# Further semaphore waits on three engines of a ReLU row-sum kernel

## The chip, the cores and the metric

The kernel runs on one core of a Trainium2 chip. The metric is the device time of one execution in microseconds (us). A core has five engines that run their own instruction streams: TensorE (PE), VectorE (DVE), ScalarE (ACT), GpSimd (POOL) and SyncE (SP). They are ordered by semaphores only: an instruction or a transfer raises a semaphore when it is done, and another engine's instruction waits until the semaphore has reached a value. Data comes from device memory (HBM) to the on-chip memory (SBUF, 128 partitions) by 16 DMA engines.

## The reference

```python
def setup_inputs():
    batch, seq, dim = 32, 512, 1024
    return {"x": np.random.randn(batch, seq, dim).astype(np.float32)}

def reference(x):
    relu_x = np.maximum(x, 0)
    return np.sum(relu_x, axis=-1).astype(np.float32)
```

The input is 16,384 rows of 1,024 float32 values (67.1 MB), the output one float32 for each row: negative values count as zero, and the row is summed.

## The kernel before

The 16,384 rows are laid out as 128 partitions with 128 rows each. Rows come in as seven chunks of 16 rows for each partition (8 MiB a chunk; the first chunk in two transfers), then a tail of 8, 4 and 2 rows, and the last two rows in four pieces (three into `buf`, one into `seam`). `buf` has three chunk buffers (`NB = 3`).

SyncE issues every transfer, from one queue. Chunks 0 to 2 are issued at once (L91), those of chunk 0 being moved ahead of the program's opening barrier (L96). For chunk c from 3 on, SyncE first waits for `s_dve` to reach `done[c - 3]` (L87), that is until VectorE's reductions of the chunk that used this buffer are done; `done` is 3, 6, 9, 12, 15, 18. The wait ahead of the tail's transfers (c = 7 in the loop) is of the same kind. A transfer raises its own semaphore `s_in[c]` by 16 when it has landed; there are 13 of these: seven chunks, three pieces of the tail, three of the last rows. Then SyncE issues the tail (L101), the last rows (L112, L115), and the three stores of results (L117, L123, L207), each behind the waits that it needs. The last line of the program, L209, waits for the stores to land.

For chunks 0 to 5, ScalarE takes most rows through a ReLU in place (L145), raising `s_act`, and VectorE sums them by a reduction over each row (L160), 18 reductions in all, each raising `s_dve` by one. Some rows of a chunk are done by one engine alone, ReLU and sum in one instruction (L127 on ScalarE, L130 on VectorE). From chunk 6 on both engines take rows in turn in this second way. A row whose values come in different pieces at the very end is put together in `seam`.

TensorE has no instruction of the kernel itself but the opening barrier's; GpSimd writes four constants and takes part in that barrier. Both are then at the end of their streams. The barrier, and what else the launch code puts in, stands under L223.

Of the kernel before, what the change touches and what calls it, by code (L numbers as in the profile page):

```python
# [6 lines left out]
NB = 3  # L7
REGIONS = [1, 111, 16]
CHUNKS = [[(0, 0, 1), (1, 0, 15)]] + [[(1, 16 * c + 15, 16)] for c in range(6)]
# [2 lines left out]
TAIL = [8, 4, 2]  # L12
CUT = 912
HEAD = 256


def bass_relu_sum_kernel(
# [19 lines left out]
    B, S, _ = x.shape  # L37
    J = B * S // P
    NBIG = len(CHUNKS)
# [12 lines left out]
    w = D - CUT  # L52
    seam = nc.alloc_sbuf_tensor("seam", [P, 2 + w + HEAD + 2], fp32)
    res = nc.alloc_sbuf_tensor("res", [P, J], fp32)
# [3 lines left out]
    s_in = [nc.alloc_semaphore(f"s_in{i}") for i in range(n_in)]  # L58
    s_act = nc.alloc_semaphore("s_act")
    s_dve = nc.alloc_semaphore("s_dve")  # L60
# [7 lines left out]
    s_out = nc.alloc_semaphore("s_out")  # L68

    sp, act, dve = nc.sync, nc.scalar, nc.vector  # L70

    NTWO = len(ACT_STEPS)
    done = [sum(map(len, DVE_STEPS[: c + 1])) for c in range(NTWO)]
# [8 lines left out]
        for i, ins in enumerate(code)  # L82
        if ins.engine == mybir.EngineType.SP and type(ins).__name__ == "InstDrain"
    )
    for c in range(NBIG + 1):
        if c >= NB:
            sp.wait_ge(s_dve, done[c - NB])  # L87
        if c < NBIG:
            i = 0
            for g, j, n in CHUNKS[c]:  # L90
                sp.dma_start(  # L91
                    out=buf[:, c % NB, i : i + n, :], in_=xv[g][:, j : j + n, :]
                ).then_inc(s_in[c], 16)
                i += n
                if c == 0:
                    code.insert(arrival, code.pop())  # L96
                    arrival += 1
    r = 0
    tail = []
    for i, n in enumerate(TAIL):  # L100
# [8 lines left out]
    flat = buf[:, tb, r : r + 2, :].rearrange("p j d -> p (j d)")  # L109
    first, second, third = [(0, CUT), (D + D // 2, 2 * D), (D + HEAD, D + D // 2)]  # L110
    for k, (lo, hi) in enumerate((first, second, third)):
        sp.dma_start(out=flat[:, lo:hi], in_=rows[:, lo:hi]).then_inc(  # L112
            s_in[NBIG + len(TAIL) + k], 16
        )
    sp.dma_start(out=seam[:, 2 : 2 + w + HEAD], in_=rows[:, CUT : D + HEAD]).then_inc(s_seam, 16)  # L115
    sp.wait_ge(s_turn, 1)
# [9 lines left out]
    def on_act(t, acc):  # L126
        return act.activation(t, t, AF.Relu, accum_out=acc)  # L127

    def on_dve(t, acc):
        return dve.tensor_scalar(  # L130
            out=t, in0=t, scalar1=0.0, scalar2=None, op0=ALU.max, op1=ALU.add, accum_out=acc
        )
# [4 lines left out]
    k = 0  # L137
# [54 lines left out]
    k = 2 + w  # L192
    lo, hi = second
    act.wait_ge(s_in[-2], 16)
    on_act(flat[:, lo:hi], seam[:, k + HEAD : k + HEAD + 1]).then_inc(s_seam, 1)
    lo, hi = third
    dve.wait_ge(s_in[-1], 16)
    on_dve(flat[:, lo:hi], seam[:, k + HEAD + 1 : k + HEAD + 2]).then_inc(s_seam, 1)
    act.wait_ge(s_seam, 16 + 2)
    act.wait_ge(s_half, 2)  # L200
    on_act(seam[:, 0:k], res[:, J - 2 : J - 1]).then_inc(s_last, 1)
    dve.wait_ge(s_seam, 16 + 2)
    on_dve(seam[:, k : k + HEAD + 2], res[:, J - 1 : J]).then_inc(s_last, 1)


    sp.wait_ge(s_last, 2)
    sp.dma_start(out=ov[-1][:, :], in_=res[:, start[-1] : J]).then_inc(s_out, 16)  # L207
# [30 lines left out]
```

## Time and profile before

| what | value |
|---|---|
| time, median of 3 runs | 160.86 us (160.74 to 161.05) |
| span of the profiled execution (first to last instruction of the program) | 159.4 us |
| instructions in the span | 150 |
| bytes read from HBM | 67.11 MB |
| ScalarE waiting for transfers at L145 | 46.1 us, 6 times |
| SyncE waiting for VectorE's reductions at L91 | 101.6 us, 4 times |
| SyncE waiting for a transfer at L122 | 31.0 us |

The span counts from the program's first instruction to its last; the time of a run is a little longer, as it holds what the launch puts around the program. An engine's busy time leaves out instructions that only wait or issue transfers, so SyncE shows no busy time at all. In the lines of the profile "q1" and "q14" are DMA queues, with packets, megabytes and the share of sixteen DMA engines' time; a name such as `SPq` or `PEldq` means an engine's sequencer, that is an instruction that waits, branches or issues. `buf<-in_x_dram` is a transfer from the input into `buf`. Lines of a timeline give the start and the length in us, the engine, the line of the kernel, the operation, what it writes and reads, and in brackets how long the engine had been idle and what ended that.

### The profile page before, as it was taken

The page shows a single profiled execution, that of the slowest core. Times are in us where ns is not written, and L with a number is a line of the kernel's source. Part 1 is how long each engine was busy: PE and PEld are TensorE (multiplying, and loading weights), DVE is VectorE, ACT ScalarE, POOL GpSimd, SP SyncE. Part 2 cuts the span into 40 slices and gives each one's busy share as a digit, 9 for nine tenths or more (in the row PEclk, how much of TensorE's full clock was granted, in tenths as well). Part 3 has the DMA queues.
Part 4 walks back from the last instruction along what each step waited for, and adds up shares of the span by engine and source line. Part 5 has one row for each costly group of instructions (what it writes and reads, how often), then busy time and mean ns, then how long its engine had stood idle before and what let it go on. Part 6 is the DMA issues. An engine that isn't in the chain of part 4 may idle for free.

```text
span 159.4 us, 150 instructions
## 1 busy us (share of the span) xinstructions
DVE 120.6 (76%) x59; ACT 101.5 (64%) x54; POOL 0.2 (0%) x4
## 2 busy tenths in 40 slices
DVE  0000000009999999999999999999999999898995
ACT  3000059980799708996099941999329980496975
POOL 0000000000000000000000000000000000000000
DMA  9997996996996997989979969969969979798994
GB/s 378 493 401 339 493 526 263 526 526 263 526 493 296 526 444 345 526 378 411 526 312 477 526 263 526 526 263 526 526 263 526 444 345 526 321 469 374 417 400 142
DMA packets 2457, 67.18 MB, mean 421 GB/s; under 512 B 536, under 2 KB 792, under 8 KB 1176
## 3 DMA queue, kind: packets, MB, share of 16 engines
q1 hardware_dynamic: 2456, 67.18, 98.1%
q14 instruction: 1, 0.01, 0.0%
HBM read 67.11 MB, written 0.07 MB: 421 GB/s over the span
## 4 chain that ended last, share of the span: by engine, by line
DVE 55%; DMA 34%; ACT 9%; SPq 2%; issue 0%
DVE res L160 54%; DMA buf<-in_x_dram 34%; ACT buf L145 9%; SPq L101 1%; SPq L112 1%; DVE buf L130 0%; DVE seam L130 0%; SPq L91 0%; DVE turned L169 0%
## 5 line engine op out<-in xcount | busy, mean ns | idle before, releaser
L160 DVE TENSOR_REDUCE res<-buf 128x4 f32<-128x4096 f32 (+3 forms) x18 | 99.4, 5596 | 35.5 <-ACT buf L145 35.5
L145 ACT ACTIVATE buf<-buf 128x7168 f32<-128x7168 f32 (+5 forms) x13 | 80.4, 6233 | 46.1 <-DMA buf<-in_x_dram 46.1
L127 ACT ACTIVATE buf<-buf 128x1024 f32<-128x1024 f32 (+2 forms) x19 | 19.0, 999 | 8.9 <-DMA buf<-in_x_dram 8.9
L130 DVE TENSOR_SCALAR_CACHE_REDUCE buf<-buf 128x1024 f32<-128x1024 f32 (+2 forms) x19 | 20.7, 1143 | 1.7 <-DMA buf<-in_x_dram 1.6
L127 ACT ACTIVATION_READ_ACCUMULATOR buf<-buf 128x1 f32 x19 | 3.6, 188 | 0.0
L145 ACT ACT_TABLE_LOAD x1 | 1.3, 1283 | 1.3 <-PEq L223 1.3
L130 DVE DVE_READ_ACCUMULATOR buf<-buf 128x1 f32 x19 | 1.6, 84 | 0.0
L130 DVE TENSOR_SCALAR_CACHE_REDUCE seam<-seam 128x258 f32<-128x258 f32 x1 | 0.4, 421 | 0.0
L127 ACT ACTIVATE seam<-seam 128x114 f32<-128x114 f32 x1 | 0.3, 300 | 0.1
L169 DVE STREAM_TRANSPOSE turned<-res 128x32 f32<-128x32 f32 x1 | 0.2, 211 | 0.0
L127 ACT ACTIVATION_READ_ACCUMULATOR seam<-seam 128x1 f32 x1 | 0.2, 186 | 0.0
L223 POOL MEMSET const-bfloat16-1.0<- 128x1 bf16 x1 | 0.1, 101 | 0.0
L223 POOL MEMSET const-uint8-127<- 128x1 uint8 x1 | 0.1, 101 | 0.0
L223 POOL MEMSET const-float32-0.0<- 128x1 f32 x1 | 0.1, 98 | 0.2 <-issue 0.2
L223 POOL MEMSET const-float32-1.0<- 128x1 f32 x1 | 0.1, 98 | 0.0
L130 DVE DVE_READ_ACCUMULATOR seam<-seam 128x1 f32 x1 | 0.1, 82 | 0.0
## 6 DMA issues: line engine op xcount, KB each, us to landing
buf<-in_x_dram SPq DMA_DIRECT2D x1, 7680.0 KB, 21.1
buf<-in_x_dram SPq DMA_DIRECT2D x1, 4096.0 KB, 25.3
buf<-in_x_dram SPq DMA_DIRECT2D x1, 2048.0 KB, 29.9
buf<-in_x_dram SPq DMA_DIRECT2D x1, 1024.0 KB, 31.9
buf<-in_x_dram SPq DMA_DIRECT2D x1, 512.0 KB, 3.3
buf<-in_x_dram SPq DMA_DIRECT2D x1, 456.0 KB, 32.5
buf<-in_x_dram SPq DMA_DIRECT2D x1, 256.0 KB, 32.7
seam<-in_x_dram SPq DMA_DIRECT2D x1, 184.0 KB, 32.6
```

What stands on the lines that cost most here:

```text
L101: sp.dma_start(out=buf[:, tb, r : r + n, :], in_=xv[-1][:, r : r + n, :]).then_inc(s_in[NBIG + i], 16)
L112: sp.dma_start(out=flat[:, lo:hi], in_=rows[:, lo:hi]).then_inc(s_in[NBIG + len(TAIL) + k], 16)
L127: return act.activation(t, t, AF.Relu, accum_out=acc)
L130: return dve.tensor_scalar(out=t, in0=t, scalar1=0.0, scalar2=None, op0=ALU.max, op1=ALU.add, accum_out=acc)
L145: act.activation(t, t, AF.Relu).then_inc(s_act, 1)
L160: dve.tensor_reduce(out=res[:, c * BIG + r : c * BIG + r + n], in_=buf[:, c % NB, r : r + n, :], axis=X, op=ALU.add,).then_inc(s_dve, 1)
L169: dve.transpose(out=turned[:, :], in_=res[:, 0:32]).then_inc(s_turn, 1)
L223: nc = _bacc.Bacc("TRN2", target_bir_lowering=False, num_devices=1)
```

## The change

A helper adds `n` waits for one semaphore and value to an engine's stream. SyncE gets 28 such calls behind the issue of each of chunks 3, 4, 5 and 6, for the value of `s_dve` that the same turn of the loop has just waited for. TensorE gets 12 for each of the 13 `s_in`, in their order, for the value that says that the piece has landed. GpSimd gets 8 for each of the 18 values of `s_dve`, in order. The compiled program has 56 to 78 further wait instructions on each of the three engines. No other instruction is added, removed or moved.

```diff
+FILL_SP = 28
+FILL_PE = 12
+FILL_POOL = 8
...
     sp, act, dve = nc.sync, nc.scalar, nc.vector
+    pe, pool = nc.tensor, nc.gpsimd
...
+    def fill(engine, n, s, v):
+        for _ in range(n):
+            engine.wait_ge(s, v)
+
     for c in range(NBIG + 1):
         if c >= NB:
             sp.wait_ge(s_dve, done[c - NB])
...
                 if c == 0:
                     code.insert(arrival, code.pop())
                     arrival += 1
+        if NB <= c < NBIG:
+            fill(sp, FILL_SP, s_dve, done[c - NB] if c >= NB else 0)
     r = 0
     tail = []
...
+    for c, s in enumerate(s_in):
+        fill(pe, FILL_PE, s, 16 * len(CHUNKS[c]) if c < NBIG else 16)
+    for k in range(done[-1]):
+        fill(pool, FILL_POOL, s_dve, k + 1)
```

## The prediction

> **What bounds the kernel now.** I began with the page's lines on DMA and the chain of work in order of time, because a kernel that reads 67 MB and writes almost nothing may simply be limited by its transfers.
>
> ```profile
> DVE 120.6 (76%) x59; ACT 101.5 (64%) x54; POOL 0.2 (0%) x4
> q1 hardware_dynamic: 2456, 67.18, 98.1%
> q14 instruction: 1, 0.01, 0.0%
> ```
>
> The reader is to see that no engine is busy for the whole span, that the data queue fills 98.1% of sixteen DMA engines' time, and that one more transfer, of instructions, lies inside the span. TensorE has no line, and GpSimd has four MEMSETs. The page's chain runs mostly over VectorE (54%), which looks as if VectorE were the limit. The timeline of ScalarE says otherwise:
>
> ```profile
> 40.97 13.95 ACT L145 ACTIVATE buf<-buf 128x7168 f32<-128x7168 f32 x2 [5.50 <-DMA buf<-in_x_dram]
> 60.31 13.95 ACT L145 ACTIVATE buf<-buf 128x7168 f32<-128x7168 f32 x2 [5.39 <-DMA buf<-in_x_dram]
> 79.67 13.95 ACT L145 ACTIVATE buf<-buf 128x7168 f32<-128x7168 f32 x2 [5.41 <-DMA buf<-in_x_dram]
> 99.02 14.04 ACT L145 ACTIVATE buf<-buf 128x4096 f32<-128x4096 f32 x3 [5.40 <-DMA buf<-in_x_dram]
> ```
>
> Every chunk of 8 MiB arrives 19.34 to 19.36 us after the one before, and ScalarE waits some 5.4 us for each: 8.389 MB / 19.35 us = 434 GB/s, or 27.1 GB/s for each of sixteen DMA engines, from about 1 us to 157 us without a hole. The end of the chain is a transfer too:
>
> ```profile
> 124.39 32.60 DMA buf<-in_x_dram
> 156.99 0.02 issue
> 157.01 0.44 DVE buf L130 x2
> 157.45 0.02 issue
> 157.47 0.43 DVE seam L130 x2
> ```
>
> So what counts is (1) anything that takes bandwidth from the stream, (2) anything that lets the stream run dry, which only SyncE can do, as it issues all transfers, and (3) what follows the last landing. Beyond the span of 159.4 us the time has 160.86 - 159.4 = 1.46 us. The records of semaphore updates in the same trace, which no view prints, show what this is: a hand-over from engine to engine at 159.51 to 159.67, resets of the semaphores by all five engines until 160.23, and a second hand-over that ends at 160.85. The last such update ahead of the program stands at -0.01, and 160.85 + 0.01 is the median, 160.86; so I take this execution's own time as 160.86, and count the hand-overs and resets.
>
> **The change, part by part.** Nothing is removed or moved. Three engines get instructions.
>
> *Number.* SyncE: 28 calls x 4 chunks = 112; TensorE: 12 x 13 semaphores = 156; GpSimd: 8 x 18 values = 144. Half of these is 56, 78 and 72, the numbers announced, so two waits share an instruction, as they do at L122 and L209. Each is worth one EVENT_SEMAPHORE:
>
> ```profile
> L223 POOLq EVENT_SEMAPHORE  x2: 17/17/17, 1.1 to 1.1; - x2
> L223 SPq EVENT_SEMAPHORE  x1: 17/17/17, 1.2 to 1.2; - x1
> L223 PEldq EVENT_SEMAPHORE  x1: 51/51/51, 1.2 to 1.2; - x1
> ```
>
> Two in a row on GpSimd start 0.08 us apart in the trace's records (1.07 and 1.15), so I take 0.08 us for SyncE and GpSimd, and 0.11 us for TensorE (its 51 ns instead of 17).
>
> *SyncE.* 14 instructions stand behind each of the issues at 52.86, 70.11, 87.58 and 104.82: 14 x 0.08 = 1.1 us. They wait for the value that the chunk's own issue has just waited for, so they only pass. Queued behind them is the wait for the next buffer, which ends 16.9 to 17.5 us after each issue. Without this cover there would still be the queue: chunk 4 is issued at 70.11 and its turn comes at 79.67, 9.6 us of slack, and more later. Cost 0.
>
> *TensorE.* It has no work; behind its waits stands only the closing hand-over. Its last six instructions wait for the last piece of buf at 156.99 and are through at 156.99 + 6 x 0.11 = 157.65. The hand-over can't be finished before SyncE has seen the last store land (the span's end, 159.4): 1.7 us of cover. Cost 0.
>
> *GpSimd.* Its last four wait for the eighteenth reduction (137.3): through by 137.6. Behind them is the hand-over again, 21 us of cover. Cost 0. No engine that computes gets an instruction, and a wait changes no semaphore, so VectorE and ScalarE have nothing more to wait for.
>
> *What is left: the code itself.* 206 instructions must be brought to the sequencers. Windows on the DMA view show how that looks. From 0 to 159 us there is q1 alone; ahead of the span there are 13 instruction packets; and the one inside lies at its very end, in a window of 20 ns (159.20 to 159.22):
>
> ```profile
> q14 instruction: 13, 0.05, 1.5%
> ...
> q14 instruction: 1, 0.01, 154.1%
> ```
>
> 154.1% of 16 x 0.02 us is 0.49 us for one packet of 8 KB (16384 GB/s in a fortieth of that window, 0.5 ns). VectorE (61 records of ours), ScalarE (57) or SyncE (22) reached that point; TensorE (2) and GpSimd (8) had not asked for any in all the 158 us that they stood. After the change they have 80 and 80, and SyncE 78: more than any engine had. If about 60 instructions made one engine fetch, all three will fetch, and in the midst of the stream: SyncE near its last fill (105 us), GpSimd near its fourteenth value of s_dve (some 110 us), TensorE near its tenth semaphore (155 us).
>
> The trace of before shows no fetch beside the stream, so its price is bounded. At the least nothing: the landings of the last piece of seam are spread over 156.98 to 157.45 by DMA engine, and a fetch on an early one disappears. One fetch that takes only its share of bandwidth on the latest engine costs 8192 B / 27.1 GB/s = 0.30 us; with the packet's own time it costs 0.49. Three on one DMA engine cost 3 x 0.49 = 1.48. A gain below nothing has no place here, since the stream has no hole to lose. The nearest rows are the single packet's two, 0.30 and 0.49, and I take the middle, 0.40 us, since three fetches on separate DMA engines delay the last landing by the latest alone.
>
> [...]
>
> *Sum.* 159.4 + 0.40 + 1.46 = 161.26 us, or 161.25.
>
> **The rivals.**
> *No change that can be measured* (within 0.2%, 0.32 us, which is about what a measurement of this kernel can tell from none). The fetches miss the stream, or land on DMA engines that finish early: 0 to 0.3 us, time 160.9 to 161.15. For it: sixteen landings spread over 0.47 us, of which only the late ones have less than 0.30 to give. Against it: three fetches, not one. I put 160.95.
>
> *Faster.* The mechanism is the fetch at the end. It runs from 159.21 to 159.70, 0.3 us past the span's end, in the midst of the hand-over. If it is SyncE's, or if an engine's closing code is late because it was not yet there, 56 to 78 more instructions have it brought during the run. The price: the 1.46 us outside the span shrink by at least 0.30 (what stands out of the span), at most by the 0.8 us between TensorE's release at 159.67 and its start of the second hand-over at 160.50. Less 0.2 for fetches in the stream, that gives 160.2 to 160.75; I put 160.35. It decides once 0.5 us are saved behind the span. For it: TensorE is, by the order of updates, the engine that opens each hand-over and the last to reset. Against it: the engines go from release to first reset in 0.11 to 0.18 us, which leaves little room for a wait for code.
>
> *Slower by a stall.* SyncE's own last instructions (the store at 157.93, the wait at L209) fall on a point where code must come, and nothing covers them: one packet, 0.49, and the some 0.9 us from SyncE's last issue (158.27) to a packet (159.21) as a delay of such a request: +1.4, 162.3. For it: SyncE would have 78 instructions, close to TensorE's 80. Against it: before, no engine shows such a stop.
>
> *The change does less than it says*: waits that are dropped as doubled. The numbers announced are exactly half of the calls, so no more than pairing was done; this goes with no change.
>
> **How the numbers follow.** Forecast (fetches cost the stream 0.3 to 0.9 us): 0.38; stall: 0.05; no change: 0.30; faster: 0.27. So slower by over 0.2% has 0.43, within 0.2% 0.30, faster 0.27. The predicted time is the forecast's 161.25. Its own range is 161.15 to 161.8. Below, the range must take in all of no change and half of faster, down to 160.2; above, it ends at 161.8, since three fetches on one engine and the stall together have less than 0.1.
>
> **What would show it.** Right: instruction packets of q14 inside the stream; chunks still 19.35 us apart but one or two of them late by 0.3 or more; the last landing near 157.8; the part outside the span still 1.46. Wrong: q14 still with one packet in the span (no change); a span of 159.4 with less than 1.2 us outside of it (faster); a gap on SyncE behind 157.4 (stall). If SyncE's issues at 70.11 to 122.07 move by more than the reductions that release them, my zero for its fills falls. If TensorE's or GpSimd's waits were found still running at 159.4, so would theirs.

## The result, and the profile after

The changed kernel takes 162.36 us (162.33 to 162.46, 5 runs) against 160.93 for the kernel before (5 runs): ratio 1.0093, 95% interval 1.0081 to 1.0105, or 1.43 us slower. The forecast was slower, 161.25 us; the measured time lies above its range.

The page of the changed kernel, in the lines that answer to those shown of before:

```profile
span 160.5 us, 356 instructions
...
DVE 120.6 (75%) x59; ACT 101.5 (63%) x54; POOL 0.2 (0%) x4
...
q1 hardware_dynamic: 2456, 67.18, 97.5%
q14 instruction: 1, 0.01, 0.0%
```

There are 206 instructions more, no engine computes longer, and there is again one instruction packet (not at the end, as before, but in the stream, as shown below). But the span is 1.1 us longer. Its end is no longer SyncE's wait for the last store: it now ends with TensorE's added waits. In the groups by source line (durations in ns, then first and last start in us), the last line of the kernel before, the same line in the changed kernel, and the added waits are these:

```profile
L209 SPq EVENT_SEMAPHORE  x1: 28/28/28, 159.4 to 159.4; - x1
```

```profile
L225 SPq EVENT_SEMAPHORE  x1: 28/28/28, 159.8 to 159.8; - x1
```

```profile
L92 PEldq EVENT_SEMAPHORE  x78: 51/51/51, 138.4 to 160.4; - x78
L92 POOLq EVENT_SEMAPHORE  x72: 42/43/43, 95.2 to 138.0; - x72
L92 SPq EVENT_SEMAPHORE  x52: 28/28/28, 53.3 to 106.0; - x52
```

L225 is the old end of the program (L209 in the kernel before). (Of SyncE's 56 further instructions four stand under L96, the line of its own wait for the next buffer.) TensorE, which computes nothing, starts its last wait at 160.4, 0.6 us after it. The same view holds the reason: TensorE's first wait is passed only at 138.4 us and GpSimd's first at 95.2, although the source gives TensorE waits from the first chunk on. TensorE's 156 waits, which nothing stands between, are 78 instructions of two, and its records show how they were paired here: the first call with the last, the second with the last but one, and so on, the innermost pair coming first. TensorE's instructions wait for semaphores (6, 6), (7, 5), (8, 4), ... (12, 0), and so 12 instructions, not 6, stand at each of the last six semaphores and none at the first six. The group narrowed to the time from 155.3 us on, when the last tail piece had landed, counts what was left:

```profile
L92 PEldq EVENT_SEMAPHORE  x48: 51/51/51, 155.3 to 160.4; - x48
```

48 in 5.1 us, 0.107 us each: from there on TensorE never waits for data, it works off a queue.

The stream is late too. ScalarE's timeline (start, length, and in brackets how long it was idle), first of the kernel before:

```profile
118.36 10.63 ACT L145 ACTIVATE buf<-buf 128x3072 f32<-128x3072 f32 x3 [5.31 <-DMA buf<-in_x_dram]
...
137.72 1.06 ACT L127 ACTIVATE buf<-buf 128x1024 f32<-128x1024 f32 x1 [6.65 <-DMA buf<-in_x_dram]
```

Then of the changed kernel:

```profile
99.18 14.04 ACT L156 ACTIVATE buf<-buf 128x4096 f32<-128x4096 f32 x3 [5.36 <-DMA buf<-in_x_dram]
118.53 10.63 ACT L156 ACTIVATE buf<-buf 128x3072 f32<-128x3072 f32 x3 [5.31 <-DMA buf<-in_x_dram]
...
138.42 1.06 ACT L138 ACTIVATE buf<-buf 128x1024 f32<-128x1024 f32 x1 [7.18 <-DMA buf<-in_x_dram]
```

Chunk 5 came 19.35 us after chunk 4, but chunk 6 took 19.89, where it had taken 19.36 before. In between lies the instruction packet, which a window of 0.1 us (137.2 to 137.3) on the DMA view finds:

```profile
q14 instruction: 1, 0.01, 19.3%
```

19.3% of 16 x 0.1 us is 0.31 us of one DMA engine. The chain ends 0.47 us later (before: 157.45 and 157.47 in the last two lines):

```profile
157.45 0.02 issue
157.47 0.45 DVE buf L141 x2
157.92 0.02 issue
157.94 0.43 DVE seam L141 x2
```

What follows the span is read from the records of semaphore updates, which no view prints. The table has us from the span's start. As these records show it, a hand-over runs from TensorE over the other engines to SyncE and back, one semaphore step each. The engines are named by the order of the steps, which is an inference; it fits that TensorE's step follows 0.19 us on its last wait in every run with waits on TensorE.

| run | last landing | SyncE's last instruction ends | TensorE opens the hand-over | SyncE's step | VectorE's step back | second hand-over ends |
|---|---|---|---|---|---|---|
| before | 157.44 | 159.39 | 1.48 | 159.51 | 159.55 | 160.85 |
| changed | 157.92 | 159.87 | 160.65 | 160.79 | 161.30 | 162.56 |
| TensorE alone | 157.50 | 159.44 | 160.22 | 160.36 | 160.87 | 162.13 |
| the same, VectorE 4 more | 157.71 | 159.68 | 160.27 | 160.41 | 160.50 | 161.77 |
| SyncE alone | 157.52 | 159.48 | 1.48 | 160.00 | 160.04 | 161.35 |
| GpSimd alone | 157.82 | 159.76 | 1.49 | 159.88 | 159.92 | 161.22 |
| fewer, TensorE in order | 157.49 | 159.44 | 158.12 | 159.55 | 159.60 | 160.86 |

Most profiled runs' own times end 0.10 to 0.12 us ahead of the last column (162.46 for the changed kernel). Three things are new in the second row: TensorE opens late, VectorE takes 0.51 us from SyncE's step to its own step back, where in the second hand-over it takes 0.10, and the last landing is late. The row with four waits more on VectorE also shows that the last landing can be some 0.25 us late without a packet in the stream, so one run's landing says little alone. The experiments take the three things apart.

### The profile page after: what moved, and what is told of

Same layout as the page of the kernel before. It is cut to its first block, busy times and chain, and to the rows that moved or that the text cites. A ratio compares the mean times of both kernels' runs of the same rounds, so it can differ in the third digit from the quotient of the medians.

```text
span 160.5 us, 356 instructions
## 1 busy us (share of the span) xinstructions
DVE 120.6 (75%) x59; ACT 101.5 (63%) x54; POOL 0.2 (0%) x4
## 4 chain that ended last, share of the span: by engine, by line
DVE 54%; DMA 34%; ACT 9%; SPq 2%; issue 0%
DVE res L171 54%; DMA buf<-in_x_dram 34%; ACT buf L156 9%; SPq L112 1%; SPq L123 1%; DVE buf L141 0%; DVE seam L141 0%; SPq L100 0%; DVE turned L180 0%; SPq L96 0%
```

## The experiments

The edits below are against the changed kernel.

**TensorE's waits alone.** `FILL_PE` stays.

```diff
-FILL_SP = 28
+FILL_SP = 0
-FILL_POOL = 8
+FILL_POOL = 0
```

> TensorE's waits alone (78 instructions), none on SyncE and GpSimd. Theory A (TensorE's queue): in the trace of the changed kernel TensorE passes 12 wait instructions for each of the last six semaphores, 0.107 us each, so from the landing of the last tail piece on (154.8 us) it has 48 to go, 5.1 us, ends near 160.0 and only then opens the closing hand-over; from its opening to the end the changed kernel needed 162.56 - 160.65 = 1.9 us. So 160.0 + 0.2 + 1.9 = 162.1 us. Theory B (the code: instruction blocks fetched in the midst of the stream): a third of the new code, a third of the loss of 1.4 us, 161.3 us.

Measured: 162.03 us, ratio 1.0072 (1.0058 to 1.0085). Theory A holds. The groups by source line:

```profile
L92 PEldq EVENT_SEMAPHORE  x78: 51/51/51, 137.8 to 160.0; - x78
```

There is no instruction packet in the stream here, and the last landing is at 157.50; yet 1.14 us of the loss are there.

**SyncE's and GpSimd's waits alone.**

```diff
-FILL_PE = 12
+FILL_PE = 0
```

> SyncE's and GpSimd's waits alone (128 instructions), none on TensorE. Theory A: TensorE's queue is gone; at most the one instruction packet seen inside the stream (at 137.2 us) is left, 0 to 0.5 us: 160.9 to 161.4 us. Theory B: two thirds of the loss stay: 161.8 us.

Measured: 161.47 us, 1.0040 (1.0027 to 1.0052). Without TensorE the largest part is gone, but 0.58 us are left, a little more than theory A had as its most. So TensorE's queue is not the whole. The trace has one packet in the stream, at 137.04 us, and 0.51 us from SyncE's last instruction to its step in the hand-over, where the kernel before has 0.12.

**All waits, TensorE's called in another order.**

```diff
-    for c, s in enumerate(s_in):
-        fill(pe, FILL_PE, s, 16 * len(CHUNKS[c]) if c < NBIG else 16)
+    landed = [(s, 16 * len(CHUNKS[c]) if c < NBIG else 16) for c, s in enumerate(s_in)]
+    for s, v in landed[::-1] + landed:
+        fill(pe, FILL_PE // 2, s, v)
```

> All waits of the change, in the same number on each engine; TensorE's are only called in another order, so that the two waits which share an instruction are for the same semaphore and there are six instructions per semaphore, from the first semaphore to the last, as the prediction had counted them. Theory A: TensorE is through at 157.45 + 12 x 0.107 = 158.7 us at the latest, ahead of SyncE, and the time is as without TensorE's waits, 160.9 to 161.4 us. Theory B: same number of instructions, same loss: 162.4 us.

Measured: 161.47 us, 1.0040 (1.0027 to 1.0052), the same as without any wait on TensorE. The number of instructions is that of the change; only the pairs differ:

```profile
L92 PEldq EVENT_SEMAPHORE  x78: 51/51/51, 21.7 to 158.2; - x78
```

The first wait is passed with chunk 0 at 21.7, the last starts at 158.2, ahead of SyncE's end. That settles it for TensorE: passed in time, its 78 instructions cost nothing here (161.47 us with them as without).

**TensorE's waits alone, doubled.**

```diff
-FILL_SP = 28
-FILL_PE = 12
-FILL_POOL = 8
+FILL_SP = 0
+FILL_PE = 24
+FILL_POOL = 0
```

> TensorE's waits alone, doubled (156 instructions, 24 for each of the last six semaphores). Theory A: 24 x 0.107 = 2.57 us per semaphore; from the landing of the 4-row piece (152.3 us) on there are 5 x 24 = 120 to go, 12.8 us, to 165.1; plus 0.2 and 1.9 as above: 167.2 us. Theory B: twice the code of TensorE alone, twice its loss: 161.8 us.

Measured: 167.35 us, 1.0404 (1.0390 to 1.0418); theory A had 167.2, theory B 161.8. Doubling the waits multiplied the loss by 5.7, as each semaphore's share is twice as long and the queue now begins a semaphore earlier:

```profile
L92 PEldq EVENT_SEMAPHORE  x120: 51/51/51, 152.6 to 165.4; - x120
```

That is the group from the 4-row piece's landing on: 120 instructions in 12.8 us. There is no packet until TensorE has passed all 156; the only one, at 166.90, comes 1.16 us after VectorE's step in the hand-over.

**GpSimd's waits alone.** What is left without TensorE, 0.58 us, was split in the same way (`FILL_SP` and `FILL_PE` at 0).

> GpSimd's waits alone (72 instructions). Theory C (a point in the code): an engine pays once, when its stream passes a certain point where the next block of code is asked for, and nothing per instruction. GpSimd passes it behind its 68th instruction, one instruction packet of 8 KB falls into the stream at some 137 us, one DMA engine ends 0.3 us late: last landing near 157.8, 161.2 us. Theory D (each added instruction costs): 0.58 us x 72/128 = 0.33, 161.2 us, without a packet in the stream. The time can't tell them apart, the trace can.

Measured: 161.15 us against 160.83, 1.0018 (1.0009 to 1.0027). The trace has the packet (DMA view, 137.1 to 137.2 us) and the late chain:

```profile
q14 instruction: 1, 0.01, 19.3%
```

```profile
157.82 0.02 issue
157.85 0.43 DVE seam L141 x2
```

Fifteen of the sixteen landings of the last piece lie at 157.11 to 157.45 and one at 157.82. So one DMA engine's last landing is 0.37 us behind the next, about the packet's 0.31 us; in the runs without a packet in the stream this distance is 0.13 us at most. GpSimd itself stops at that point: its waits start 0.087 us apart, but 0.43 us lie between the 68th and the 69th instruction (132.20 us). Nobody waits for GpSimd, so this stop costs nothing.

**GpSimd's waits alone, doubled** (`FILL_POOL = 16`).

> GpSimd's waits alone and doubled (144 instructions, 152 in all on GpSimd). [...] Theory D: twice the loss, 161.55 us.

Measured: 161.20 us, 1.0019 (1.0010 to 1.0028): the same loss for twice the instructions. One packet again, now at 115.27 us, 5.1 us behind the 68th instruction (110.18). Theory C as put for GpSimd's waits alone, paid once and not for each instruction, fits; D falls.

**SyncE's waits alone** (`FILL_PE` and `FILL_POOL` at 0).

> SyncE's waits alone (56 instructions). Theory C: no packet in the stream, last landing at 157.45 as before, but 0.5 us instead of 0.12 from SyncE's last instruction to its hand-over, since the point in the code lies behind its 78th and last instruction: +0.4, 161.3 us. Theory D: 0.58 x 56/128 = 0.25, 161.15 us.

Measured: 161.23 us, 1.0026 (1.0017 to 1.0034). From 0 to 159 us the DMA view has data alone, and the stream ends as before, but the table has 0.52 us from SyncE's last instruction to its step, against 0.12.

```profile
q1 hardware_dynamic: 2446, 67.18, 98.3%
```

```profile
157.52 0.02 issue
157.55 0.43 DVE seam L141 x2
```

So with 28 calls a chunk the program's end falls on SyncE's point in the code, and there nothing covers the stop of 0.4 us.

**SyncE's waits alone, 32 calls a chunk and 26.**

> SyncE's waits alone, 32 for each chunk (64 instructions, 86 in all). Theory C: the point behind the 78th instruction now lies among the issues of the last rows at 124 us, whose transfers have some 13 us until their turn, so the pause costs nothing and the hand-over comes in 0.12 us; but the packet falls into the stream at some 128 us and one DMA engine ends 0.3 us late: 161.15 us. Theory D: 0.40 x 64/56 = 0.46, 161.3 us, no packet in the stream, and a hand-over 0.5 us late.

With 32: 161.09 us, 1.0013 (1.0004 to 1.0022). The stop shows in the chain, behind the 79th instruction, where an issue takes 0.04 us otherwise; its time is covered, and the packet (129.69 us, 0.31 us long) costs the stream about what it cost with GpSimd:

```profile
124.43 0.42 issue
124.86 32.39 DMA buf<-in_x_dram
157.25 0.02 issue
157.27 0.46 DVE buf L141 x2
157.73 0.02 issue
```

> SyncE's waits alone, 26 for each chunk instead of 28 (52 instructions, 74 in all). Theory C: the program ends four instructions ahead of SyncE's point: 160.85 us, 0.12 us from SyncE's last instruction to its hand-over. Theory D: 0.40 x 52/56 = 0.37, 161.2 us.

With 26, theory C missed: 161.20 us (160.81 to 161.73), 1.0022 (1.0011 to 1.0034), which is the number that theory D had. Yet none of the places known so far shows the loss: no packet was in the stream, SyncE's step came 0.14 us after its last instruction, and the second hand-over ended at 160.91, 0.06 later than before. The profiled run's time, 161.15, is 0.24 us past that end, where the other profiled runs stand 0.10 to 0.13 ahead of it, so some 0.35 us were lost behind the last recorded update. A stop that has moved by four instructions to that place would fit the time. It doesn't fit the packet, which stands at 160.98: in the other runs, where the DMA engines were idle, it came 1.1 to 1.4 us after a stop began, so this one would have begun at 159.6 to 159.9, ahead of SyncE's step in the second hand-over (160.70). The cause of this run's loss stays open. A price for each added wait does not explain it either: with 32 calls theory D had 161.3 and 161.09 was measured, and with 24, next, there is no loss at all.

**All three engines with fewer waits, TensorE's in order.** Beside TensorE's other order:

```diff
-FILL_SP = 28
+FILL_SP = 24
-FILL_POOL = 8
+FILL_POOL = 6
```

> All three engines get waits, with TensorE's in the order of the semaphores (78 instructions), SyncE's 24 for each chunk instead of 28 (48 instructions, 70 in all on SyncE), GpSimd's 6 for each value instead of 8 (54, 62 in all). Theory C: neither SyncE nor GpSimd reaches its point within the program, TensorE is through in time: 160.9 us, no loss with 180 of the 206 instructions. Theory D: 0.58 x 102/128 = 0.46, 161.35 us.

Measured: 160.79 us against 160.83, 0.9998 (0.9989 to 1.0006). 180 of the 206 instructions, and no loss. The groups by source line:

```profile
L92 PEldq EVENT_SEMAPHORE  x78: 51/51/51, 21.5 to 157.9; - x78
L92 POOLq EVENT_SEMAPHORE  x54: 42/43/43, 95.0 to 137.7; - x54
L92 SPq EVENT_SEMAPHORE  x44: 28/28/28, 53.2 to 105.8; - x44
```

GpSimd ends with its 62nd instruction, SyncE with its 70th, both short of their points; from 0 to 159.3 us there is no instruction packet.

**TensorE's waits alone, and four more instructions at VectorE's end.** VectorE's half microsecond between its two steps was the last piece without a cause.

```diff
     for k in range(done[-1]):
         fill(pool, FILL_POOL, s_dve, k + 1)
+    fill(dve, 8, s_last, 2)
```

> TensorE's waits alone, as in the first experiment (162.03 us), and four wait instructions on VectorE behind its last one, for a semaphore that is set by then. In the first experiment VectorE took 0.54 us from its step in the closing hand-over to its next one, against 0.12 in the second hand-over. Theory C: this is VectorE's point in the code, right behind its last instruction; before, it lay beside the wait for the last store, and now, as TensorE opens the hand-over late, nothing covers it. Four instructions more put it ahead of VectorE's step, into the time in which it waits for TensorE: -0.4, 161.6 us. Rival: the 0.54 us belong to a late opening as such: 162.0 us, or 0.2 more for the waits.

Measured: 161.65 us, 1.0046 (1.0032 to 1.0059); 0.38 us are won by adding instructions. VectorE's four:

```profile
L92 DVEq EVENT_SEMAPHORE  x4: 49/50/50, 158.2 to 159.0; - x4
```

The records put the starts at 158.23, 158.34, 158.85 and 158.95: 0.10 us apart, and 0.52 in the middle. The stop is in VectorE's own code now, while it waits for TensorE, and its step back in the hand-over comes after 0.10 us. So a late opening alone doesn't make it, and theory C's place is right.

## Why the prediction was right or wrong

*What bounds the kernel: right.* The stream still sets the pace; a packet of 0.31 us on one DMA engine came out at the end as 0.21 to 0.37 us (three runs without TensorE's waits).

*Number of instructions: right.* 56, 78 and 72, in pairs. Which waits share an instruction was taken as the source order has it, and that was wrong.

*SyncE's fills, cost 0: right as far as they are passed, wrong at the end.* They pass in 0.06 us each (0.08 was taken), and the issues move by some 0.1 us under cover: the one at 70.11 comes at 70.23, while the reduction that releases it ends 0.05 later. By the prediction's own sign (issues that move by more than their reductions) its zero would fall; but with 24 calls there is no loss, so the queue's slack covers this. But SyncE's longer code brings its stop of 0.4 us to the program's end: 0.40 us alone. In the changed kernel this hides behind TensorE: SyncE's last instruction ends at 159.87, and 0.52 us later, at 160.39, VectorE's step that SyncE needs (160.76) is still to come. It is the rival "slower by a stall" in mechanism and place, priced 1.4.

*TensorE, "through at 156.99 + 6 x 0.11 = 157.65 ... Cost 0": the step that failed.* The price of one was right (0.107 us). The count was not: pairs of first and last put 12 at each of the last six semaphores, 1.3 us of work each, and from the last tail piece on the landings are 0.3 to 1.1 us apart, so they pile up. The prediction had named the sign, TensorE's waits still running at 159.4, and it came. TensorE ends at 160.46 and opens the hand-over 1.14 us after SyncE had been ready to follow it in the kernel before (160.65 against 159.51). By the runs: 0.77 us for the late opening alone (161.65 against 160.88), and 0.38 more, since VectorE's own stop, which had lain beside the wait for the last store, is no longer covered. The prediction knew of no such stop; it shows in the part outside the span, 162.46 - 160.46 = 2.00 us instead of 1.46.

*GpSimd, cost 0: right for the engine.* Its waits, late by the same pairing, are through at 138.0.

*The code: mechanism right, number and size off.* One packet fell into the stream, not three: GpSimd's. There it took 0.31 us, not the 0.49 of the packet at the end, and it costs 0.32 us (161.15 against 160.83) where 0.40 was taken. TensorE asked for none, in 80 instructions or in 158, and SyncE's comes after the stream. So the forecast's own mechanism gives less than a quarter of the 1.43 us; that the direction came out owes more to TensorE's queue, which the prediction had at nothing.

The sum of the runs, 0.77 + 0.38 + 0.32 = 1.47, stands against 1.43 measured. SyncE's 0.40 is not in it, as it is hidden. The packet's 0.32 is in it although TensorE ends last, because TensorE's queue starts from a landing: that of the last tail piece comes at 155.32 instead of 154.89 with TensorE's waits alone, and the queue ends at 160.46 instead of 160.03. Without TensorE's waits the two parts, 0.32 + 0.40 = 0.72, stand against 0.58 measured (0.43 to 0.84 by its interval).

*The rivals.* "No change" fell. "Faster" fell: no variant was shown to be faster than the kernel before. That the part outside the span shrinks did happen where four more instructions moved VectorE's stop ahead, but only as TensorE had uncovered that stop (0.38 us). The packet at the end of the kernel before, which "faster" and "stall" thought might be SyncE's, is by its time VectorE's: it starts 1.15 us after VectorE's step in the hand-over (158.06), and with TensorE's waits alone the packet starts 1.29 us after that step (160.33). "Still one packet in the span", the sign for no change, came true and misled, as it was another packet. Last, 160.86 as this execution's own time from the last update is 0.1 too long by the later profiles.

What an engine does at such a stop, no run shows. GpSimd's (0.34 us, which nobody waits for) and SyncE's with 32 calls a chunk (0.38 us) were covered; the packet in the full stream (0.32 us) and the stop at the program's end (0.40 us) were not.

## What to carry to other kernels

In these runs an engine without work still took part in the hand-over that ended the program, so its last instruction counted: TensorE, which computes nothing, opened the hand-over 0.19 us after its last wait. A wait instruction that was already satisfied took 0.06 to 0.107 us, and a dozen per event made a queue where events followed each other within 1.3 us (12 x 0.107). Read from the compiled order, or from when each wait is first passed, which waits share an instruction; here the source order did not tell. And in this program, which fills its DMA engines, code had a place as well as a length: with 64 instructions more SyncE's stop was under cover and a packet in the stream (161.09 us), with 56 the stop lay on the program's end (161.23), and with 48, beside fewer waits on GpSimd and TensorE's in order, there was no loss (160.79). The place could not always be foretold: with 26 calls on SyncE it was not where four instructions fewer should have put it.

## What the hardware showed that was not expected

- An engine's stop at a certain point of its code, 0.34 to 0.42 us beyond its usual pace: GpSimd behind its 68th recorded instruction (in every run that reaches it), SyncE behind its 78th or 79th, VectorE behind its 63rd (the one run that has so many). TensorE showed none in 158.
- The packet of 8 KB came 1.1 to 1.4 us after such a stop began when the DMA engines were idle (SyncE alone: 159.48 to 160.60; VectorE, with TensorE's waits alone: 160.33 to 161.62, in the changed kernel: 160.76 to 162.15) and 4.8 to 5.3 us after it in the stream (GpSimd alone: 132.20 to 137.12; SyncE with 32 calls: 124.43 to 129.69). The engine had gone on long before, so the stop of 0.4 us was not a wait for that packet.
- A satisfied wait instruction took 0.060 us on SyncE, 0.087 on GpSimd, 0.10 on VectorE and 0.106 on TensorE, start to start.
